# A hybrid mLSTM and Hyena block on one core: operand places of the MLP opened at the start, heads begun beside the last values matmuls, and a new order at the border to the output projection

## The chip, the cores and the metric

The kernel runs on one core of a Trainium2 chip. The metric is device time in microseconds (us) of one execution; before the change three runs took 2702.84, 2704.43 and 2706.27, so the median is 2704.43. The engines are called by their short names: PE (TensorE, matmuls), DVE (VectorE), ACT (ScalarE), POOL (GpSimd) and SP (SyncE, which here only issues loads).

## What the kernel computes

One encoder layer over 2048 positions and 1024 channels in fp32. One projection feeds two groups of 512 channels. Group A is a bidirectional mLSTM with 4 heads of 128 channels, computed in 16 chunks of 128 positions; group B is an order-2 Hyena operator, two long convolutions with gates. Both are normalised per group, joined, projected by `w_out`, normalised and added to the input; a squared-ReLU MLP follows.

```
proj  = rms_norm(x, norm_mix_pre) @ w_in
cv    = short_conv3(proj[:, :N_CONV])              # q, k, hyena v, x1, x2
q, k  = silu(cv[q]), silu(cv[k]) / sqrt(128)       # 4 heads each
v, o  = proj[v], sigmoid(proj[o])
h_m   = (mlstm(q, k, v, gates) + reversed(mlstm(reversed ...))) * o
y_m   = group_rms(h_m, 4)
# mlstm, per chunk: C <- decay*C + (w*k)^T v ;  num = ((q k^T) * wts) v + scale * (q C)
#                   out = num / max(|den|, exp(-m))
z     = cv[x1] * fftconv(cv[hv], filt1);  z = cv[x2] * fftconv(z, filt2)
y_h   = group_rms(z, 8)
x     = x + rms_norm(concat(y_m, y_h) @ w_out, norm_mix_post)
x     = x + rms_norm(relu(rms_norm(x) @ w_mlp_in)^2 @ w_mlp_out, norm_mlp_post)
```

## The kernel before

A fp32 matmul of large size is three matmuls of rounded halves (`mm3`, L159 to L161); the halves are made by ACT (the rounded high part) and DVE or POOL (the rest), in `split` (L166, L169). Small products (mLSTM, transposes) are single fp32 matmuls.

The stages follow one another: normalisation and filters (to 260 us), the first long convolution beside the convolved projections (to 640), the second beside the values projection (to 1024), the mLSTM (to 1168), the output projection (to 1440) and the MLP.

*The stages up to 1024 us* run under a fixed order: every engine takes its instructions as the program writes them. `drive` lets the long convolution lead: each `yield n` of `hyena` asks for n us of projection work, which `convolved` and then `values_project` give in pieces (`yield 1.4` is twelve matmuls, half of a 128x260 tile). Three `yield 1.3` stand in each of its 32 steps j. `values_project` takes four groups of 260 columns in the order 3, 0, 1, 2, each for 16 row tiles t; the normalised input `hn` lies in SBUF for it in four blocks b of 512 rows. Of group 2 (the last) all columns pass a sigmoid on ACT on their way to `vst` and to DRAM `vo`. After the second convolution the lead waits (`yield 14`, then for the gates) and turns head 0's `k`.

*The mLSTM* (`mlstm`, L881) is written as a loop over n = 16 h + ch, and a scheduler places its instructions on each engine. Per chunk there are the score matmul `pS` (L990), the two weight masks `mb` (loaded and broadcast from DRAM `mrow`, cut by POOL at L980 and L981, exponentiated by ACT at L993), their product `pm` on DVE, and, five chunks later, the state product `ps` (L1008) and the two value products `pa` (L1010); ACT scales `ps` into `nm` (L1015), DVE adds `pa`. After each four chunks POOL divides and adds the directions (`ht`, L1028 and L1030), and ACT's queue stores `ym`. Each head needs four groups of transposes `ptk` (L945) with scalings `kw` and fifteen state steps `pv` (L966) first; those of head h+1 stand inside head h. PSUM has five banks for `pv`, `ps`, `pa`, three others for `ptk` and `pS`. The loads of `k`, `q`, `v` are issued by the table `LOADS`; `loads_ahead` loads `w_out` and the data of two gates, `first_gate` makes row tile 0's Hyena half of the output projection's input.

*The output projection* (`out_proj`, L1319) has 16 row tiles of 128 rows. Each takes 48 matmuls `po`: 24 for its Hyena half (`y`, from `gate` and `turned`), 24 for its mLSTM half (`ym`, from `mixed`: POOL's product with the output gate, squares on ACT, sums on DVE, POOL's scaling, transposes). Its opening splits the eight blocks of `w_out` (`weight`, L1339) and prepares rows 0 and 1. From then on a fixed order holds, which works three row tiles at a time.

*The MLP* reads its operands from places `hm<i><e>` of 8 KB per partition, in a pool that is opened after the mLSTM.

## Time and profile before

| | us |
|---|---|
| median of three runs | 2704.43 |
| the profiled execution | 2700.58 |
| its span | 2698.5 |
| PE busy | 2598.6 (96%) |
| DVE, ACT, POOL busy | 1541.0, 1230.1, 1206.1 |
| 0 to 1024 us, PE busy | 994.88 of 1024 |
| 1024 to 1196 us, PE busy | 141.60 of 172 |
| 1196 to 1440 us, PE busy | 236.72 of 244 |
| 1440 to 2698 us, PE busy | 1225.36 of 1258 |

The busy times of the stages are sums of windows of the trace. Times of single instructions are read from the profiled execution, whose clock starts at its first instruction; they carry over to the median only as differences. PE's matmuls overlap by a little, so the spacing of starts tells more than the length of one.

### The profile page before, as it was taken

Reading aid. Unit: us, or ns where it says so; the run is one execution under the profiler, and the core shown is the slowest. Engines: PE = TensorE matmul, PEld = TensorE weight load, DVE = VectorE, ACT = ScalarE, POOL = GpSimd, SP = SyncE. Lnnn points to the kernel's source line nnn. Section 1 sums busy time; section 2 is a strip of 40 time slices with the busy share of each in tenths; the row PEclk is TensorE's granted clock in tenths of the full one; section 3 lists DMA queues with packets and bytes.
Section 4 is the critical chain, followed back from the end, with each engine's and each line's share of the span. In section 5 each row is a group of like instructions: output and inputs, shape, how many; then the busy total and the mean of one; then the engine's idle time right before and its main releaser. Section 6 shows DMA issues by size and latency. Waiting matters only on the chain.

```text
span 2698.5 us, 35390 instructions
## 1 busy us (share of the span) xinstructions
PE 2598.6 (96%) x12237; PEld 2109.2 (78%) x12237; DVE 1541.0 (57%) x2454; ACT 1230.1 (46%) x2292; POOL 1206.1 (45%) x964
## 2 busy tenths in 40 slices
PE   6999999999999998879997999999999999999998
PEld 4778888777798888757774788868888888888876
DVE  5676653777556666656556444474444433543477
ACT  6355544555544446643334444454544333232344
POOL 1211114555225543456667877687772340301232
PEclk9999999999999999899999999999999999999999
DMA  6233336666676658546755444555447453445555
GB/s 173 56 93 110 113 117 216 187 196 187 198 237 180 197 167 272 183 152 213 245 186 210 156 141 163 185 190 172 144 156 282 146 181 98 129 144 160 183 168 214
DMA packets 288354, 465.74 MB, mean 173 GB/s; under 512 B 37542, under 2 KB 149414, under 8 KB 287152
## 3 DMA queue, kind: packets, MB, share of 16 engines
q1 hardware_dynamic: 227600, 324.85, 39.0%
q10 hardware_dynamic: 53264, 117.53, 11.4%
q0 software_dynamic: 7312, 21.11, 3.1%
q8 instruction: 97, 1.59, 0.2%
q14 instruction: 81, 0.66, 0.1%
HBM read 289.27 MB, written 174.13 MB: 172 GB/s over the span
## 4 chain that ended last, share of the span: by engine, by line
PE 39%; DVE 4%; POOL 4%; issue 3%; DMA 2%; ACT 2%; ACTq 0%; DVEq 0%; SPq 0%; POOLq 0%
PE pm L159 13%; PE pm L160 13%; PE pm L161 13%; DMA m<-in_w_mlp_out_dram 1%; POOL xt L1255 1%; DVE cb L169 1%; POOL cb L169 1%; ACT xo L1395 1%; DVE hm L1892 0%; DVE hm L169 0%; DVE xo L1398 0%; DMA hm<-ht 0%; DVE gss L1297 0%; POOL ht L1430 0%; DVE hm L1822 0%
## 5 line engine op out<-in xcount | busy, mean ns | idle before, releaser
L166 ACT CAST cb<-m 128x1024 fp32r<-128x1024 f32 (+1 forms) x342 | 277.4, 846 | 441.3 <-PE pm L159 386.2
L169 DVE TENSOR_TENSOR cb<-m,cb 128x1024 fp32r<-128x1024 f32 (+1 forms) x222 | 237.3, 1106 | 303.1 <-ACT cb L166 302.6
L160 PE MATMUL pm<-cb 128*128 128x512 f32 x880 | 343.4, 390 | 7.8 <-DVE cb L169 7.8
L159 PE MATMUL pm<-cb 128*128 128x512 f32 x880 | 342.3, 389 | 1.3 <-DVE cb L169 1.0
L159 PE MATMUL pm<-hm,cb 128*128 128x512 f32 x840 | 331.4, 394 | 12.3 <-DVE m L1703 6.4
L161 PE MATMUL pm<-cb 128*128 128x512 f32 x880 | 342.5, 389 | 0.0
L160 PE MATMUL pm<-hm,cb 128*128 128x512 f32 x840 | 330.2, 393 | 2.5 <-POOL hm L169 2.5
L161 PE MATMUL pm<-hm,cb 128*128 128x512 f32 x840 | 329.7, 393 | 0.0
L169 POOL TENSOR_TENSOR cb<-m,cb 128x1024 fp32r<-128x1024 f32 x120 | 266.1, 2230 | 57.5 <-ACT cb L166 57.5
L1703 DVE TENSOR_TENSOR m<-pm,m 128x512 f32<-128x512 f32 x224 | 153.9, 690 | 229.4 <-PE pm L161 220.5
L159 PE MATMUL pt<-hn,w 128*128 128x512 f32 x640 | 269.5, 421 | 1.0 <-ACT hn L486 0.9
L160 PE MATMUL pt<-hn,w 128*128 128x512 f32 x640 | 253.9, 397 | 0.7 <-DVE hn L487 0.7
L161 PE MATMUL pt<-hn,w 128*128 128x512 f32 x640 | 253.0, 395 | 0.0
L169 POOL TENSOR_TENSOR raw<-raw,hi 128x512 fp32r<-128x512 f32 x160 | 206.1, 1301 | 99.7 <-ACT hi L166 74.8
L160 PEld LDWEIGHTS pm<-cb 128*128 128x128 f32 x880 | 165.2, 188 | 45.7 <-DVE cb L169 11.7
L159 PEld LDWEIGHTS pm<-hm,cb 128*128 128x128 f32 x840 | 159.2, 189 | 49.0 <-POOL cb L169 7.6
L159 PEld LDWEIGHTS pm<-cb 128*128 128x128 f32 x880 | 165.1, 188 | 36.5 <-ACT junk L1877 1.4
L161 PEld LDWEIGHTS pm<-cb 128*128 128x128 f32 x880 | 165.2, 188 | 33.9
L160 PEld LDWEIGHTS pm<-hm,cb 128*128 128x128 f32 x840 | 159.4, 190 | 37.4 <-POOL hm L169 2.9
L161 PEld LDWEIGHTS pm<-hm,cb 128*128 128x128 f32 x840 | 159.2, 190 | 34.2
L1707 ACT ACTIVATE m<-m 128x512 f32<-128x512 f32 x128 | 80.7, 630 | 229.1 <-DVE m L1703 221.7
L635 POOL DMA_DIRECT2D vp<-vst x96 | 61.2, 642 | 231.7 <-ACT vst L631 230.6
(320 smaller groups left out, 5725.6 us busy)
## 6 DMA issues: line engine op xcount, KB each, us to landing
ga<-m ACTq DMA_DIRECT2D x96, 512.0 KB, 3.6
m<-ga SPq DMA_DIRECT2D x96, 512.0 KB, 3.8
d<-st ACTq DMA_DIRECT2D x64, 512.0 KB, 3.2
m<-in_w_mlp_in_dram SPq DMA_DIRECT2D x64, 512.0 KB, 5.7
m<-in_w_mlp_out_dram SPq DMA_DIRECT2D x114, 256.0 KB, 4.0
raw<-d SPq DMA_DIRECT2D x96, 256.0 KB, 2.9
xt<-in_x_dram SPq DMA_DIRECT2D x32, 512.0 KB, 3.9
dk<-kst SPq DMA_DIRECT2D x32, 512.0 KB, 4.0
```

Source lines behind the costliest of these rows:

```text
L159: pe.matmul(ps, w[1], x[0], start=first, stop=False)
L160: pe.matmul(ps, w[0], x[1], start=False, stop=False)
L161: pe.matmul(ps, w[0], x[0], start=False, stop=last)
L166: self.act.copy(hi, src)
L169: (eng_lo or self.dve).tensor_tensor(lo, src, hi.bitcast(F32), ALU.subtract)
L635: pool.dma_start(dst[:, 8 * b + e:8 * b + 8:2, cc:cc + 128], st[64 * e:64 * e + 64])
L1255: eng.tensor_tensor(res[:, cs], tmp[e], res[:, cs], ALU.add)
L1395: act.activation(x1, xt, AF.Square, accum_out=ss1[:, h:h + 1])
L1703: dve.tensor_tensor(dst, a, b, ALU.add)
L1707: act.activation(g, g, AF.Relu)
```

## The change

Eight of the MLP's operand places (`hm40` to `hm71`, 8 KB each) are opened at the start of the kernel and first hold blocks 0 and 1 of `hn` (now in halves of 4 x 512). When the last values group has used a block, its places take `k`, `q`, `v` and masks of heads 0 and 1, then, inside the mLSTM, operands of head 3, and half of `w_out`. The loads for that stand beside the last values group, at tiles 4 to 15. The transposes, the fifteen state steps and the first scores of head 0 stand there too. The cover of the long convolutions is 1.2 instead of 1.3. In the mLSTM masks are loaded three quads (four chunks each) ahead, and the tables `TURNS`, `WEIGHTS`, `AHEAD` and `GATES` say at which n transposes, splits of `w_out`, loads and two gates come. The opening of the output projection gets a fixed order. Line numbers of the kernel after the change are larger (`ptk` L968, `pv` L989, `pS` L1023, exponentials L1026, `ps` L1041, `pa` L1043, `nm` L1048, sigmoids L736).

```diff
+            self.hq = c.enter_context(tc.tile_pool(name="hq", bufs=1, reuse_waits="tile"))
-            self.hn = [[hp.tile([128, 8, 512], F32R, name=f"hn{b}{e}") for e in range(2)] for b in range(4)]
+            self.hn = [[[self.place(t) for t in tags[2 * e:2 * e + 2]] for e in range(2)]
+                       for tags in (("60", "61", "50", "51"), ("70", "71", "40", "41"))]
+            for b in range(2, 4):
+                self.hn.append([[hp.tile([128, 4, 512], F32R, name=f"hn{b}{e}{j}") for j in range(2)] for e in range(2)])
...
@@ long_conv, after hyena
-        self.mh = [{} for _ in range(4)]
-        self.head_loads(0, "kvq")
-        yield 14.0
-        while not self.gates_done:
-            yield 1.0
-        for g in (0, 3, 1, 2):
-            self.turned(0, g)
-            yield 2.5
+        yield 1.4
+        for i, g in enumerate((0, 3, 1, 2)):
+            self.turned(0, g, ("kt", "s")[i % 2])
+            yield 1.4
+        for step in range(15):
+            self.state_step(0, step, self.mps0, ("s", "kt")[step % 2])
+            yield 1.4
+        for n in range(4):
+            self.scores(0, n)
+            yield 1.4
@@ values_project
+        first = {4: (self.head_loads, 0, "k"), 5: (self.head_loads, 0, "v"), 6: (self.weights_load, 0), 7: (self.head_loads, 0, "q"),
+                 8: (self.weights_load, 1), 9: (self.head_loads, 1, "k"), 10: (self.masked, 0), 11: (self.head_loads, 1, "v"),
+                 12: (self.masked, 1), 13: (self.weights_load, 2), 14: (self.weights_load, 3), 15: (self.head_loads, 1, "q")}
...
+            if g == order[-1] and t in first:
+                first[t][0](*first[t][1:])
@@ mlstm
-        LAG, AHEAD = 5, 10
-        LOADS = {1: "v1", 5: "q1", 9: "k2", 14: "v2", 19: "q2", 32: "k3", 32 + LAG: "v3", 40: "q3"}
+        LAG = 5
+        LOADS = {4: (2, "k"), 8: (2, "v"), 12: (2, "q"), 28: (3, "v"), 32: (3, "k"), 37: (3, "q")}
...
+        GATES = {58: (0, 0), 59: (1, 0), 60: (0, 1), 61: (1, 1), 64: (0, 2), 66: (0, 3), 67: (1, 3)}
-        for step in range(15):
-            self.state_step(0, step)
-        for n in range(64 + LAG):
+        for n in range(4, 64 + LAG):
...
-            while ready < 16 and ready <= (n + AHEAD) // 4:
-                self.weights(*divmod(ready, 4))
+            if n % 4 == 1 and 4 <= n // 4 + 3 < 16 and n > 8:
+                self.weights_load(n // 4 + 3)
...
+            if n % 4 == 3 and n // 4 + 1 < 16:
+                self.masked(n // 4 + 1)
+            if n in WEIGHTS:
+                self.weight(4 + WEIGHTS.index(n))
@@ hyena, three times in a step
-                    yield 1.3
+                    yield 1.2
@@ new: the split of a block of w_out, now also called inside the mLSTM
+    def weight(self, k):
+        hi, lo = (e[:, k % 2, :] for e in self.wos[k // 2])
+        wf = self.ahead.pop(k)
+        self.act.activation(hi, wf, AF.Copy, scale=self.yw[:, k:k + 1])
+        self.dve.scalar_tensor_tensor(lo, wf, self.yw[:, k:k + 1], hi.bitcast(F32), ALU.mult, ALU.subtract)
@@ out_proj, opening
-        for k in (4, 5, 6, 7):
-            weight(k)
-            if k == 5:
-                zs[1] = gate(1)
...
-        ym = {0: turned(mixed(0), 0, 1)}
-        for k in range(4):
-            weight(k)
+        with tc.manual_schedule(engines={mybir.EngineType.PE,mybir.EngineType.DVE,mybir.EngineType.Activation}):
+            opened[2] = opening(2)
+            tiles = mixed_loads(0)
+            pos[0], pos[1] = banks(0), banks(1)
+            for k in (4, 5, 6, 7):
+                weight(k - 4)
+                for i in range(2):
+                    for e in range(2):
+                        part(pos[i], e, yz[i], 4, (k - 4,))
+                if k == 5:
+                    zs[2] = gate(2)
+            yz[2] = yz[0]
+            self.turn_split(ps.tile([128, 512], F32, tag="tp", name="ptp", bufs=3), zs.pop(2), yz[2])
+            pos[2] = [self.h1p.tile([128, 512], F32, tag="h1", name="po1"), ps.tile([128, 512], F32, tag="tp", name="po2", bufs=3)]
+            for e in range(2):
+                part(pos[2], e, yz[2], 4)
+            ym = {0: turned(mixed(0, tiles), 0, 1)}
```

The order on PE at the end of the values projection (`pt`), before:

```order
L160 MATMUL pt_10305<-w1_9562,hn30_94 128x260
L161 MATMUL pt_10305<-w0_9561,hn30_94 128x260
L945 MATMUL ptk_10335<-eye_62,k_10286 128x128 x4
L945 MATMUL ptk_10347<-eye_62,k_10286 128x128 x4
L966 MATMUL pv_10428<-v_10288,kw0_10340 128x129
L966 MATMUL pv_10433<-v_10288,kw0_10340 128x129
L966 MATMUL pv_10438<-v_10288,kw0_10340 128x129
L966 MATMUL pv_10443<-v_10288,kw0_10340 128x129
L945 MATMUL ptk_10359<-eye_62,k_10286 128x128 x4
L966 MATMUL pv_10428<-v_10288,kw1_10353 128x129
```

and after the change, first a state step of head 0 with the next piece of the values matmuls behind it:

```order
L989 MATMUL pv_10458<-hm50_10045,kw0_10211 128x129
L989 MATMUL pv_10458<-hm50_10045,kw1_10185 128x129
L159 MATMUL pt_10443<-w0_9733,hn311_105 128x260
L160 MATMUL pt_10443<-w1_9734,hn301_103 128x260
L161 MATMUL pt_10443<-w0_9733,hn301_103 128x260
```

The end of the values matmuls after the change, further down on the same engine:

```order
L160 MATMUL pt_10443<-w1_9738,hn301_103 128x260
L161 MATMUL pt_10443<-w0_9737,hn301_103 128x260
L989 MATMUL pv_10478<-hm50_10045,kw0_10159 128x129
L989 MATMUL pv_10478<-hm50_10045,kw1_10134 128x129
L989 MATMUL pv_10485<-hm50_10045,kw0_10159 128x129
L989 MATMUL pv_10485<-hm50_10045,kw1_10134 128x129
L989 MATMUL pv_10490<-hm50_10045,kw0_10159 128x129
L989 MATMUL pv_10490<-hm50_10045,kw1_10134 128x129
L1023 MATMUL pS_10495<-hm61_10126,hm60_10003 128x128 x4
L968 MATMUL ptk_10548<-eye_62,hm70_10231 128x128 x3
L1023 MATMUL pS_10539<-hm61_10126,hm60_10003 128x128 x2
L968 MATMUL ptk_10548<-eye_62,hm70_10231 128x128
```

Before, head 0's transposes, all its state steps and its scores come behind the last `pt`. After, three state steps and the scores are what is left of it there; `ptk_10548`, from `hm70`, is already head 1's.

The order on ACT at the same place, before, from the last store of the convolution (`d21`) on:

```order
L234 DMA d21_3601<-st_10228 128x1024
L720 ACTIVATE vst_10245<-pt_10232 128x260
L720 ACTIVATE vst_10318<-pt_10264 128x260
L720 ACTIVATE vst_10318<-pt_10305 128x260
L950 ACTIVATE kw0_10340<-ptk_10335,qt_3582 128x128 x4
L950 ACTIVATE kw0_10352<-ptk_10347,qt_3582 128x128 x4
L950 ACTIVATE kw0_10364<-ptk_10359,qt_3582 128x128 x4
L950 ACTIVATE kw0_10376<-ptk_10371,qt_3582 128x128 x4
L993 ACT_TABLE_LOAD
L993 ACTIVATE mb_10407<-mb_10407,qt_3582 128x128 x8
```

and after:

```order
L1026 ACT_TABLE_LOAD
L1026 ACTIVATE hm51_10084<-hm51_10084,qt_3592 128x128
L973 ACTIVATE kw0_10184<-ptk_10179,qt_3592 128x128 x4
L736 ACT_TABLE_LOAD
L736 ACTIVATE vst_10204<-pt_10140 128x260
L973 ACTIVATE kw0_10211<-ptk_10206,qt_3592 128x128 x4
L736 ACTIVATE vst_10204<-pt_10191 128x260
L1026 ACT_TABLE_LOAD
L1026 ACTIVATE hm51_10084<-hm51_10084,qt_3592 128x128 x4
L736 ACT_TABLE_LOAD
L736 ACTIVATE vst_10296<-pt_10241 128x260
L1026 ACT_TABLE_LOAD
```

The exponentials (of `hm51`, where the masks of quads 0 and 1 lie) have moved between the sigmoids of the last values tiles (`vst`), and a table load stands at each change between them; there are 13 in the tail, where one stood before.

The order on PE at the mLSTM's end, before; `xg0` and `rda` are the Hyena halves of rows 0 and 1, `po0` and `po1` banks of the output projection:

```order
L1008 MATMUL ps_11917<-st_11385,q_11419 128x258
L1010 MATMUL pa_11918<-v_11316,pm_11858 128x129 x2
L1306 MATMUL pty_11922<-eye_62,xg0_10395 128x128 x4
L1290 MATMUL py_11976<-rda_11742,s1i_3586 128x512
L159 MATMUL po0_11992<-wo0_11960,y01_10397 128x512
L159 MATMUL po1_11993<-wo0_11960,y01_10397 128x512
L160 MATMUL po0_11992<-wo1_11961,y00_10396 128x512
L161 MATMUL po0_11992<-wo0_11960,y00_10396 128x512
```

The same place after the change:

```order
L1043 MATMUL pa_11930<-v_11146,pm_11888 128x129 x2
L1350 MATMUL pty_11934<-eye_62,xg0_10525 128x128 x4
L1041 MATMUL ps_11944<-st_11401,hm71_11328 128x258
L1043 MATMUL pa_11945<-v_11146,pm_11888 128x129 x2
L1350 MATMUL pty_11949<-eye_62,rda_11753 128x128 x4
L1041 MATMUL ps_11960<-st_11401,hm71_11328 128x258
L1043 MATMUL pa_11961<-v_11146,pm_11888 128x129 x2
L159 MATMUL po0_12012<-hm60_11362,y01_10521 128x512
L160 MATMUL po0_12012<-hm61_11363,y00_10520 128x512
L161 MATMUL po0_12012<-hm60_11362,y00_10520 128x512
```

Before, row 1's gate (`py`) and the first block of w_out stand at the border; after, both rows' transposes stand in front of the last `pa` and row 0's matmuls directly behind it. Where row 0's mLSTM half (`yt`, from `ymt`) begins, before:

```order
L160 MATMUL po1_12027<-wo1_11963,yt_12018 128x512
L161 MATMUL po1_12027<-wo0_11962,yt_12018 128x512
L1306 MATMUL ptp_12066<-eye_62,ymt_12052 128x128 x4
L1290 MATMUL py_12114<-rd_12109,s1i_3586 128x512 x2
L159 MATMUL po0_11992<-wo0_11964,yt_12065 128x512
L160 MATMUL po0_11992<-wo1_11965,yt_12065 128x512
```

and after:

```order
L159 MATMUL po2_12093<-hm50_11364,y01_10521 128x512
L160 MATMUL po2_12093<-hm51_11365,y00_10520 128x512
L161 MATMUL po2_12093<-hm50_11364,y00_10520 128x512
L1350 MATMUL ptp_12128<-eye_62,ymt_12008 128x128 x4
L159 MATMUL po0_12012<-hm70_11995,yt_12127 128x512
L160 MATMUL po0_12012<-hm71_11996,yt_12127 128x512
```

Before, the transposes of `ymt` stand behind row 1's Hyena half (`po1_12027`), and after behind row 2's (`po2_12093`).

## Rows read from the trace of the kernel before

**Rows 1.** windows: length, busy us of five engines, clock, DMA share, GB/s
```profile
640.00:1024.00 384.00, 379.22 (x2315) 326.20 (x2313) 236.56 (x423) 179.35 (x362) 156.64 (x155) 1.00 0.63 194
1024.00:1044.00 20.00, 14.32 (x94) 13.29 (x93) 10.94 (x35) 11.71 (x38) 3.73 (x7) 0.83 1.00 325
1044.00:1168.00 124.00, 107.78 (x728) 97.09 (x729) 84.27 (x229) 82.28 (x286) 60.98 (x62) 0.94 0.60 187
1168.00:1196.00 28.00, 19.50 (x67) 13.99 (x66) 17.64 (x22) 12.95 (x19) 12.63 (x8) 0.82 0.61 189
1196.00:1385.00 189.00, 187.70 (x871) 145.40 (x870) 109.16 (x193) 73.12 (x183) 118.14 (x107) 1.00 0.66 216
```

**Rows 2.** timeline of PE: start us, us, instruction, [idle before <- releaser]
```profile
1023.39 0.28 PE L161 MATMUL pt<-w,hn 128*128 128x260 f32 x1
...
1043.93 0.67 PE L1008 MATMUL ps<-st,q 128*128 128x258 f32 x2 [1.60 <-DVE st L971]
```

**Rows 3.** timeline of TensorE, a stretch of the mLSTM without waits
```profile
1067.41 0.60 PE L1008 MATMUL ps<-st,q 128*128 128x258 f32 x2
...
1068.52 0.60 PE L1008 MATMUL ps<-st,q 128*128 128x258 f32 x2
```

**Rows 4.** timeline of TensorE, just after it in the mLSTM
```profile
1078.40 0.60 PE L945 MATMUL ptk<-eye,k 128*128 128x128 f32 x4
1078.84 0.61 PE L966 MATMUL pv<-v,kw 128*128 128x129 f32 x4
1079.29 0.39 PE L990 MATMUL pS<-q,k 128*128 128x128 f32 x2
1083.10 1.23 PE L1008 MATMUL ps<-st,q 128*128 128x258 f32 x2 [3.43 <-ACT nm L1015]
```

**Rows 5.** waits from 1023 to 1165 us: us in total, times, longest
```profile
POOL mb L980 <- DMA mb<-mrow: 42.1, 9, 22.0
...
ACT nm L1015 <- POOL ht L1030: 18.4, 8, 4.3
```

**Rows 6.** groups by line, 1023 to 1168 us: busy us, mean ns, idle
```profile
L993 ACT ACTIVATE mb<-mb,qt 128x128 f32<-128x128 f32 x128 | 42.4, 405 | 9.1 <-POOL mb L980 3.7 <-POOL ht L1030 3.3 <-DVE st L971 2.1
...
L1015 ACT ACTIVATE nm<-ps,qt 128x129 f32<-128x129 f32 x126 | 38.9, 373 | 29.7 <-POOL ht L1030 18.4 <-PE ps L1008 9.7 <-PE pa L1010 1.6
...
L950 ACT ACTIVATE kw<-ptk,qt 128x128 f32<-128x128 f32 x64 | 18.3, 376 | 9.8 <-PE ptk L945 9.7
```

**Rows 7.** timeline of ScalarE at the first exponentials
```profile
1036.71 1.28 ACT L993 ACT_TABLE_LOAD   x1
1038.00 4.20 ACT L993 ACTIVATE mb<-mb,qt 128x128 f32<-128x128 f32 x14
```

**Rows 8.** timeline of TensorE from the mLSTM's end into the output projection
```profile
1165.06 1.02 PE L1290 MATMUL py<-rda,s1i 128*128 128x512 f32 x2
...
1166.82 0.61 PE L1010 MATMUL pa<-v,pm 128*128 128x129 f32 x4
...
1180.38 0.40 PE L160 MATMUL po<-wo,y 128*128 128x512 f32 x1
1180.61 0.39 PE L161 MATMUL po<-wo,y 128*128 128x512 f32 x1
...
1185.65 0.80 PE L159 MATMUL po<-wo,yt 128*128 128x512 f32 x1 [4.21 <-DVE yt L169]
...
1193.72 0.60 PE L1306 MATMUL ptp<-eye,ymt 128*128 128x128 f32 x4
...
1195.72 0.55 PE L159 MATMUL po<-wo,yt 128*128 128x512 f32 x1
```

**Rows 9.** timeline of GpSimd, the first normalised ymt
```profile
1186.95 1.99 POOL L1300 TENSOR_TENSOR ymt<-ymt,gr_r 128x512 f32<-128x512 f32 x1 [2.11 <-DVE gr_r L241]
```

**Rows 10.** timeline of VectorE in the second hyena pass
```profile
1005.16 0.68 DVE L1147 TENSOR_TENSOR z<-pu,z 64x512 f32<-64x512 f32 x1 [2.96 <-PE pu L161]
...
1011.70 0.68 DVE L1147 TENSOR_TENSOR z<-pu,z 64x512 f32<-64x512 f32 x1 [2.96 <-PE pu L161]
```

211 lines of the change are left out of this document (111 added, 100 removed).

## The prediction

> **What bounds the kernel now.** I read the windows first, stage by stage [rows 1]. From 640 to 1024 us TensorE is busy 379.22 of 384 us, and in the projection loop after 1196 it is busy 187.70 of 189: both are bound by TensorE. Between them it is not. From 1024 to 1044 it works 14.32 of 20 us with a granted clock of 0.83, from 1044 to 1168 107.78 of 124 at 0.94, from 1168 to 1196 19.50 of 28 at 0.82. Only these 172 us can give anything back, and of the two levels (1.2 and 2.4 GHz) the lower one is in force in part of each.
>
> Then TensorE's timeline at the border [rows 2]: the last matmul of the values projection starts at 1023.39, the first `ps` of the mLSTM at 1043.93. In a run without waits one chunk (pS, ps, pa) costs 1068.52 - 1067.41 = 1.11 us [rows 3]; a group of four transposes `ptk` costs 0.44 and a state step (a pair of `pv`; a step and a group stand in a row) 1078.84 to 1079.29, so 0.45 [rows 4]. The next row there is a `ps` that came 3.43 us late for ACT's `nm`, and it ran 1.23 us where the same shape took 0.60: a stall is paid a second time in the clock. What ACT waited for stands in the table of waits [rows 5]: `nm` waits 18.4 us for GpSimd's `ht`, and GpSimd's masks `mb` wait 42.1 us for their loads, 22.0 of them once, at the start.
>
> **The change, part by part.** *Head 0 beside the last values.* In before all of the mLSTM's TensorE work lies between 1023.5 and the end of the last `pa`, 1166.82 + 0.45 = 1167.3 [rows 2, 8]: 143.8 us. The work is 64 chunks x 1.11 = 71.0, 16 groups of transposes x 0.44 = 7.0, 60 state steps x 0.45 = 27.0 and two gates' `py` at 1.02 [rows 8] = 2.0: 107.0 us, so 36.8 us are lost to waits and the lower clock. After the change 4 groups and 12 of head 0's 15 steps stand between the values' matmuls, where TensorE is full: the values end 4 x 0.44 + 12 x 0.45 = 7.2 us later, at 1030.7. What is left behind is 71.0 + 12 x 0.44 + 48 x 0.45 + 2.9 (two gates with their transposes) = 100.8 us. With no loss the last `pa` ends at 1131.5, 35.8 us earlier; with the old loss at 1168.3, 1.0 later. Neither end is likely. For a gain speaks that the 22.0 us wait for the first masks falls before the values' end, and that the other 20 us of mask waits, which stand behind ACT's 18.4, go when masks are fetched three quads ahead and masked one quad ahead. Against the whole of it speaks ACT's own work [rows 6]: 120 of 128 exponentials (39.8), all `nm` (38.9), three quarters of `kw` (13.7), together 92.4 us, and the casts of half of w_out and of two gates on top: about as much as TensorE's 100.8. Two queues equally full, that wait on each other every chunk, lose something. I take half of the old loss, 18.4 us: last `pa` at 1150, a gain of **17** (-1 to 36).
>
> *Table loads.* The order shows 12 more table loads on ACT in the values' tail, since the exponentials of head 0 now alternate with the sigmoids of the last values. One took 1.28 us and the first exponential started at its end [rows 7]: 12 x 1.28 = 15.4 us of ACT. ACT evicts one 260-wide tile for each 3 to 4 us of TensorE there, so I cost them at nothing on TensorE's path before the border and count what ACT still owes at it into the half loss above; without that cover they cost up to 15.4. The Trainium skill, "ScalarE: Activation LUTs", section "What ACT_TABLE_LOAD costs", gives about 1283 ns for the load and 1380 ns of drain; the trace agrees on the load and shows no drain in front of the exponential. By that page 12 switches would be an estimated 32 us of ACT, 16.6 more for rival C, and the rule to do all of one table set before switching, in its section "Rules for kernel authors", speaks against this order.
>
> *Opening of the output projection.* From the last `pa` (1166.82) to row 0's first mLSTM-half matmul (1195.72) before takes 28.9 us [rows 8]. Half of w_out and both first gates now are split inside the mLSTM, so the 48 matmuls of rows 0 and 1 follow the last `pa` at once, and 24 of row 2 with their transposes come behind. What then is late is the chain of the last `ym`: GpSimd's normalised `ymt` is done at 1186.95 + 1.99 = 1188.94 [rows 9], 22.1 us behind the last `pa`. From the transposes of `ymt` to row 0's matmul it takes 1195.72 - 1193.72 = 2.00 [rows 8], so that matmul starts 24.1 us behind the last `pa`, 4.8 earlier. In that time 24 x 0.23 = 5.5 us of row 2 (1180.38 to 1180.61, the spacing of `po` [rows 8]) are done in addition, which the full loop then banks. Gain **10**. ACT still has the squares of the second `ymt` in front of the cast that row 2 needs (this order made before wait 4.21 us for `yt` [rows 8]): if row 2 slips behind the chain, only 4 remain; if the chain itself, relieved of four splits on VectorE and ACT, shortens by some 6, 16.
>
> *Cover in the long convolution.* 1.2 instead of 1.3 per third of a step keeps up to 0.3 us x 64 = 19 us of projection work for later. It is the same work, so its place costs nothing if TensorE doesn't wait. VectorE's product chain repeats every 1011.70 - 1005.16 = 6.54 us and waits 2.96 us of it for TensorE's `pu` [rows 10]: it has ten times the 0.3 to give. Cost 0, at worst 19. Loads, the doubled mask of one quad, and the split operand places cost nothing: more DMAs on SP's queue, but they come at the end of the hyena's own loads, and TensorE's queue there holds values matmuls whose operands are in place.
>
> **The sum.** 17 + 10 = 27 us off the profiled execution, whose span of 2698.5 makes 2700.58 us: 2673.6. It lies 3.85 under the median of the three runs, so on the median scale 2704.43 - 27 = 2677.
>
> **The rivals.** *A, the work changes its place and the loss stays.* The mLSTM loses 36.8 us as before, since it is ACT and VectorE that are full. For it: ACT's 92.4 us and more. Against: the named waits for masks. Only the opening is gained: 2704.4 + 1.0 - 10 = 2695.
>
> *B, the stalls vanish.* A loss of 5 us and the short chain: 31 + 14 = 45 us, 2659. Against it stands ACT again.
>
> *C, slower: ACT's queue at the border.* In the tail ACT runs in order through exponentials of masks that are loaded late there (the order has quads 2 and 3 behind the stores of vst), each between two table loads. If a mask comes as late as the first one in before, 22.0 us, ACT's sigmoids, `kw` and `nm` stand behind it, and 15.4 us of loads with them: up to 37.4 us, that TensorE can't bridge, since its banks for `ps` are freed by ACT's `nm` alone. From 27 us of ACT's lag it is a loss; at its full size 2677 + 37 = 2714. Against: TensorE reads no sigmoid, and the masks' loads move out of the 20 us in which the DMA engines were full (share 1.00) into a stage at 0.63 [rows 1].
>
> *D, the cover was needed.* Each hyena step waits for what it lost: up to 19 us, 2696. Against: the 2.96 us of slack above.
>
> **How the numbers follow.** Forecast 2677 with chance 0.52 (its own range 2666 to 2690: losses of 8 to 28 us, with openings of 10 and 6). A 0.17, B 0.08, C 0.10, D 0.13. 0.2% of the time, 5.4 us, is about what can be told from no change. Faster: all of the forecast and B, most of A (9 us, 0.145) and of D (0.10): 0.85. Same: what is left of A and D with a small C, 0.07. Slower: C and the worst of D, 0.08. Leaving 0.1 out above and 0.1 below, the range is 2662 to 2698.
>
> **What would show it.** Right: a first `ps` within 3 us of the last values matmul, at about 1033; the last `pa` near 1150; waits of GpSimd's masks far under 42 us; row 0's mLSTM half some 24 us behind the last `pa`, with row 2's hyena half in front of it; hyena steps of about 6.25 us without new waits. Wrong: a last `pa` beyond 1160 (A), TensorE waiting for `nm` behind table loads around 1035 (C), waits for `pu`, `pi` or `py` between 300 and 1000 us (D), or the MLP's 1258 us changed, on which I count nothing.

## The result: slower by 0.3%, where 1% faster was forecast

The changed kernel takes 2712.68 us (median of 8 runs, 2711.35 to 2717.36), the kernel before beside it 2706.09 (8 runs, 2701.78 to 2707.16). The ratio is 1.0029 with a 95% interval of 1.0019 to 1.004. The forecast was 2677, with a range of 2662 to 2698.

The profiled execution has a span of 2709.8 us against 2698.5, so 11.3 more; the medians are 6.6 apart, so a single pair of traces holds some us of scatter. The windows of the kernel after, same columns as [rows 1]:

```profile
640.00:1024.00 384.00, 378.69 (x2304) 326.15 (x2303) 238.79 (x435) 189.24 (x384) 155.59 (x154) 1.00 0.65 204
1024.00:1044.00 20.00, 15.15 (x117) 14.43 (x116) 7.91 (x19) 16.77 (x32) 4.26 (x10) 0.93 0.80 255
1044.00:1168.00 124.00, 107.12 (x732) 94.90 (x731) 90.06 (x239) 86.93 (x286) 63.85 (x59) 0.98 0.58 175
1168.00:1196.00 28.00, 21.58 (x84) 16.25 (x84) 7.92 (x11) 5.83 (x10) 9.27 (x8) 0.88 0.48 161
1196.00:1385.00 189.00, 182.66 (x841) 141.84 (x840) 107.37 (x191) 73.37 (x183) 116.67 (x106) 0.98 0.65 213
```

The three windows that could give something back run at a higher clock, as meant, and two of them are a little fuller (the one from 1044 to 1168 is not: 107.12 against 107.78). But the loop after 1196, full before (187.70 of 189), is not any more (182.66). A table by fixed times does not show the rest, so I cut the trace at TensorE's own marks: the end of the last values matmul, the end of the last `pa`, the start of TensorE's first `pm` (the MLP's matmuls; VectorE's `pm` in the mLSTM is another tile), the end of the last `pm`. Worked out from the traces, in us, differences from unrounded times:

```
                          before    after    difference
values end                1023.7   1031.8       +8.1
values end -> last pa      143.8    129.6      -14.1
last pa -> first pm        249.0    253.2       +4.1
first pm -> last pm       1272.7   1285.9      +13.2
rest                         9.3      9.3        0
```

So the mLSTM gains 14.1 us behind the values' end, 8.1 of which the values pay, 4.1 are lost again in the output projection, and 13.2 in the MLP, whose code the change does not touch.

TensorE at the border in after (start, us, instruction, [idle before <- releaser]), to be held against [rows 2, 8]:

```profile
1031.52 0.28 PE L161 MATMUL pt<-w,hn 128*128 128x260 f32 x1
...
1034.83 0.60 PE L1041 MATMUL ps<-st,hm 128*128 128x258 f32 x2
...
1041.88 1.23 PE L1043 MATMUL pa<-hm,pm 128*128 128x129 f32 x4 [3.35 <-DVE pm L1029]
...
1160.84 0.61 PE L1043 MATMUL pa<-v,pm 128*128 128x129 f32 x4
```

The first `ps` comes 3.3 us behind the last values matmul instead of 20.5, but the first `pa` only 10.1 us behind the values' end: it needs the product `pm` of the scores and masks of chunks 0 to 3, and so their exponentials. ScalarE there, first its timeline, then the mask's cut on GpSimd and the product on VectorE:

```profile
1020.57 0.39 ACT L736 ACTIVATE vst<-pt 128x260 f32<-128x260 f32 x1 [1.17 <-issue]
1026.30 1.28 ACT L1026 ACT_TABLE_LOAD   x1 [5.34 <-DMA hm<-mrow]
1027.59 0.40 ACT L1026 ACTIVATE hm<-hm,qt 128x128 f32<-128x128 f32 x1
1028.01 1.28 ACT L736 ACT_TABLE_LOAD   x1
1029.31 0.39 ACT L736 ACTIVATE vst<-pt 128x260 f32<-128x260 f32 x1
...
1036.83 1.28 ACT L1026 ACT_TABLE_LOAD   x1
1038.12 2.44 ACT L1026 ACTIVATE hm<-hm,qt 128x128 f32<-128x128 f32 x8
```
```profile
1026.35 0.64 POOL L1013 TENSOR_SCALAR_AFFINE_SELECT hm<-hm 128x512 f32<-128x512 f32 x1 [19.12 <-DMA hm<-mrow]
```
```profile
1040.60 1.23 DVE L1029 SCALAR_TENSOR_TENSOR pm<-pS,hm 128x1024 f32<-128x1024 f32 x1 [3.29 <-ACT hm L1026]
```

That is rival C in small: a mask comes late (5.34 us), sigmoids and exponentials alternate, and 13 table loads of 1.28 us stand between 1005 and 1038. The late mask is that of chunk 8, and the eight exponentials of chunks 0 to 3 are the last row of ScalarE: in its order they stand behind those of chunks 4 to 9, though the first `pa` needs them first. The waits from 1023 to 1165 us, as in [rows 5]:

```profile
POOL hm L1013 <- DMA hm<-mrow: 19.1, 1, 19.1
POOL mb L1013 <- DMA mb<-mrow: 13.3, 4, 4.9
...
ACT nm L1048 <- POOL ht L1063: 9.1, 5, 2.3
PE pa L1043 <- ACT nm L1048: 8.2, 8, 1.8
```

ScalarE's wait for `ht` halved (18.4 to 9.1). It did not vanish, and what it really is comes below.

### The profile page after: what moved, and what is told of

Same layout as the page of the kernel before. It is cut to its first block, busy times and chain, and to the rows that moved or that the text cites. A ratio compares the mean times of both kernels' runs of the same rounds, so it can differ in the third digit from the quotient of the medians.

```text
span 2709.8 us, 35397 instructions
## 1 busy us (share of the span) xinstructions
PE 2606.8 (96%) x12237; PEld 2108.6 (78%) x12237; DVE 1552.2 (57%) x2453; ACT 1242.7 (46%) x2303; POOL 1209.3 (45%) x964
## 3 DMA queue, kind: packets, MB, share of 16 engines
q10 hardware_dynamic: 53264, 117.53, 11.3%
## 4 chain that ended last, share of the span: by engine, by line
PE 39%; DVE 4%; POOL 4%; DMA 3%; issue 3%; ACT 2%; ACTq 0%; SPq 0%; DVEq 0%; POOLq 0%
PE pm L159 13%; PE pm L161 13%; PE pm L160 13%; DVE cb L169 1%; POOL xt L1288 1%; POOL cb L169 1%; DMA hm<-ht 1%; ACT xo L1448 1%; DVE hm L1946 0%; POOL ht L1483 0%; DVE gss L1341 0%; DMA m<-in_w_mlp_in_dram 0%; DVE m L1757 0%; DVE xo L1451 0%; DVE hm L169 0%
## 5 line engine op out<-in xcount | busy, mean ns | idle before, releaser
L646 POOL DMA_DIRECT2D vp<-vst x96 | 61.2, 642 | 233.0 <-ACT vst L642 231.9
L612 DVE SCALAR_TENSOR_TENSOR yc<-pt,cw,yc 128x511 f32<-128x511 f32 (+1 forms) x280 | 135.1, 516 | 45.2 <-ACT yc L606 43.1
L1861 POOL TENSOR_TENSOR m<-m,hm 128x512 f32<-128x512 f32 x32 | 50.1, 1568 | 241.1 <-DMA m<-in_w_mlp_out_dram 230.1
L159 PE MATMUL pt<-hm,w 128*128 128x512 f32 x320 | 133.2, 416 | 0.9 <-ACT hm L494 0.9
```

The costliest lines, as they stand in the source:

```text
L159: pe.matmul(ps, w[1], x[0], start=first, stop=False)
L612: dve.scalar_tensor_tensor(y[:, at], p[:, src], cw[:, ct, w:w + 1], y[:, at], ALU.mult, ALU.add)
L646: pool.dma_start(dst[:, 8 * b + e:8 * b + 8:2, cc:cc + 128], st[64 * e:64 * e + 64])
L1861: pool.tensor_tensor(b[:, 0], b[:, 0], t2[s], ALU.subtract)
```

## Experiments

Two theories stood at the start. Theory 1: the MLP's 13 us come from the tiles' new addresses; its rival: from the new order, by way of the clock or of transfers. Theory 2: the mLSTM's gain fell short for the masks' late loads; its rivals: the table loads, ScalarE's work, and the queues. Times are of the slowest core, "before" is the kernel before, run beside it. As a first finding of all these runs together: the time of the values' end differs between kernels whose code up to there is the same (1023.1 to 1027.9 in seven built on before, 1031.8 to 1037.5 in five that are after up to there), so stages are compared by their length and not by times from the start. The lengths scatter too. Where the code of a stage is after's, the stretch from the values' end to the last `pa` takes 129.6 to 132.9 us, and the MLP at after's addresses 1281.7 to 1286.8. Runs for which no interval is given are single executions.

**b_layout: before with after's addresses.** The change has two side effects on SBUF: the decay tile went from the right-hand side into the constants on the left (128 bytes more there), and two operand places of the MLP became 8256 bytes wide, for v with its 129th column.

```diff
-            self.cp_bg = cp.tile([128, 16], F32, name="bg")
-            self.cw = cp.tile([128, 20, 4], F32, name="cw")
+            t = cp.tile([128, 128], F32, name="cw")
+            self.cp_bg, self.cw = t[:, 80:96], t[:, 0:80].rearrange("p (t n) -> p t n", n=4)
+            self.decay = t
...
-        wos = {j: [wp.tile([128, 2, D], F32R, tag=f"hm{i}{e}", ...
+        wos = {j: [wp.tile([128, 2, D] if e or i > 5 else [128, 16, 129], F32R, tag=f"hm{i}{e}", ...
```

> The kernel before with one thing changed: its MLP tiles lie at the SBUF addresses that they have after the change (the shared cw/bg/decay tile at the bottom, two operand places of 8256 instead of 8192 bytes, so that operands, raw ring and split weights move by 128 to 512 bytes). Order and work are those of before. Theory 1 (the addresses slow the MLP's up steps): an up step of 84 matmuls takes 19.3 to 19.5 us instead of 19.05, the MLP is 7 to 9 us longer over its 32 up steps, and the whole run is 6 to 11 us slower than before. Rival (the MLP is slower because of what the new order leaves behind: stalls, clock, queues): 19.05 us a step and a time within 3 us of before.

Measured: 2714.94 against 2705.41, ratio 1.0035 (1.0024 to 1.0047). Its MLP takes 1284.1 us, and its matmuls have after's spacing to the tenth of a nanosecond. Addresses alone, with before's order of instructions, are as slow as the whole change.

**b_decay: the decay tile alone.**

> The kernel before with only the decay tile moved into the shared tile at the bottom: left-hand tiles (operands hm4 to hm7, hm3, ring) 128 bytes up, right-hand tiles (split weights, hm1, hm2) 512 bytes up. Theory 1: the up steps leave 19.05 us if distances between left and right tiles matter (they change by 384 bytes); they stay if only the widened places matter. Rival: 19.05 us, time as before.

Measured: 2712.74; MLP 1283.0. The 128 bytes of the decay tile are enough, with another pattern of slow products.

**a_right256: after with 256 bytes of padding on the right** (one unused tile under places 1 and 2).

> The changed kernel with a pad of 256 bytes in front of the right-hand MLP tiles, so that ring and split weights have the distance of the kernel before again (modulo 512 bytes), and hm3 too; hm4 to hm7 have not. Theory 1 in the form 'ring against split weights': up steps back to 19.05 to 19.15 us and the run 6 to 9 us faster than the changed kernel (2704 to 2707). In the form 'hm4 to hm7 against something': steps stay at 19.4 and the time at 2712. Rival (order, not addresses): 19.4, 2712.

Measured: 2715.82, ratio to before 1.004 (1.0025 to 1.0054), the spacing as after's. I took it for proof that right-hand addresses don't count. That was too quick: 256 turned out to be the one padding that can't show anything.

**a_masks: after with the mask rows loaded earlier** (rows 2 and 3 at tiles 9 and 11, head 1's k and v behind them).

> The changed kernel with the loads of masks 2 and 3 four and three tiles earlier (tiles 9 and 11 of the last values group) and head 1's k and v later (13 and 14). Theory 2 (ACT stood 5.3 us behind a late mask in the values' tail, and TensorE then 1.5 + 3.4 us behind ACT, at a lower clock): those waits at 1037 to 1042 us go and the last pa is 4 to 8 us earlier. Rival (the mLSTM is full on ACT and VectorE, so it is given back): the last pa is less than 2 us earlier. Either way the MLP is as in the changed kernel.

Measured: 2716.96, ratio 1.0039 (1.0024 to 1.0054); 132.3 us from the values' end (1035.35) to the last `pa` against 129.6. No gain. ScalarE's longest wait for a mask in the tail is 1.58 us now, and yet the first `pa` comes 9.2 us behind the values' end. On ScalarE, VectorE and TensorE:

```profile
1040.75 2.44 ACT L1026 ACTIVATE hm<-hm,qt 128x128 f32<-128x128 f32 x8
```
```profile
1043.22 1.22 DVE L1029 SCALAR_TENSOR_TENSOR pm<-pS,hm 128x1024 f32<-128x1024 f32 x1 [2.37 <-ACT hm L1026]
```
```profile
1044.50 0.71 PE L1043 MATMUL pa<-hm,pm 128*128 128x129 f32 x4 [2.43 <-DVE pm L1029]
```

The exponentials of chunks 0 to 3 are again the last of the tail, now behind those of chunks 4 to 12. Theory 2 falls in this form: the late mask alone does not hold the start.

**b_ring256, b_hm128, a_ring256: which tile?** One unused tile ahead of the ring of result tiles, or ahead of the operand places:

```diff
+            mk.tile([128, 64], F32, tag="pad", name="pad")          # b_ring256, a_ring256
+            self.hq.tile([128, 32], F32, tag="pad", name="pad")     # b_hm128
```

> Kernel before with one unused 256-byte tile ahead of the MLP's ring of result and weight tiles, so that this ring alone lies 256 bytes higher (at the address it has after the change); operand places, constants and right-hand tiles stay. Theory ring (the distance between ring and other tiles sets the spacing of the up steps' matmuls): products 1, 2, 6, 5, 7 of the first 16 steps go from 226.7 to some 231 to 233 ns, time about 2713 (+7 to +9). Theory places (the moving operands' own address does): spacing as before (226.7, with 5 at 228.2 and 7 at 232.4), time about 2705.

> Kernel before with one unused 128-byte tile ahead of the operand places, so that places 3 to 7 and the ring behind them lie 128 bytes higher; constants and right-hand tiles stay. Theory places and theory ring both: as the run that moved the decay tile alone, products 1, 2, 6 at 233.3 and 5 at 232.4 ns, time about 2712. Rival (the constants' tiles, which that run moved too, or the right-hand side): spacing as before, about 2705.

> Kernel after with the same 256-byte tile ahead of the ring, which then stands at its address of before plus 512 bytes. Theory ring, if the address counts modulo 512: spacing of before comes back, time about 2704 (-9). Theory places: spacing as after, about 2713.

Measured: b_ring256 2707.4 with before's spacing, a_ring256 2714.11 with after's, b_hm128 2711.76 with b_decay's. The ring is out; the moving operands' places are what counts. Sorting the up steps' matmuls by product (mean spacing in ns, steps 3 to 14, 12 matmuls of 512 columns each; in brackets the address of the place, high and low part, in bytes modulo 256; the stationary weights stand at 160 in all but b_right128, where they stand at 32):

```
product      1           2           6           5           7           4           3
before       227.9 (160) 226.7 (160) 226.7 (160) 226.7 (160) 226.7 (160) 226.7 (160) 232.6 (32)
b_hm128      226.7 (160) 226.7 (160) 232.6 (32)  233.3 (32)  233.3 (32)  233.3 (32)  227.9 (160)
after        230.8 (160) 226.7 (160) 232.6 (32)  231.7 (32,96) 232.9 (96) 233.0 (96,160) 231.7 (32)
b_right128   226.7 (32)  226.7 (32)  232.6 (160) 233.3 (160) 233.3 (160) 233.3 (160) 227.9 (32)
a_align      226.7 (160) 226.7 (160) 226.7 (160) 226.7 (160) 226.7 (160) 226.7 (160) 226.7 (160)
```

A product is fast where its moving and its stationary operand stand at the same byte modulo 256, and slow where they don't; the first two or three matmuls of a product still show the one before it (227.9). Two things do not fit a rule of each matmul by itself: product 1 of after has both at 160 and takes 230.8, slow in ten of its matmuls behind the slow product 3; and in its product 4 the four matmuls that read the low part, at 160 like the weights, take 234.8 ns on the mean, no less than the eight that read the high part at 96. Why stays open. The last two rows were run to test the sentence.

**b_right128 and a_align.** 128 bytes on the right-hand side of before move weights and places 1 and 2 to 32; in a_align all places and the weights of after stand at 160 (two unused 64-byte tiles; place 40 first, its operand 64 bytes into the slot). b_align is before with 128 bytes ahead of place 3.

```diff
+            hm = {t: self.place(t) for t in ("40", "60", "61", "51", "70", "71", "41", "50")}   # a_align
...
+            t = self.hq.tile([128, 2064], dtype, tag="hm40", name="hm40")[:, 16:2064]
```

> Kernel before with one unused 128-byte tile on the right-hand side, so that the split weights (the up steps' stationary operands) and places 1 and 2 go from 160 to 32 bytes modulo 256; places 3 to 7 stay (place 3 at 32, the others at 160). Theory pair (a matmul is slow where its moving and its stationary operand lie at different bytes modulo 256): products 6, 5, 7, 4 go to 232 to 233 ns, 1, 2 and 3 to 226.7; up steps some +0.2 us each, time about 2712. Theory moving (a moving operand at 32 is slow wherever the weights are): products 1, 2, 3 at 232 to 233, 6, 5, 7, 4 at 226.7; time about 2709.

> Kernel before with one unused 128-byte tile ahead of place 3, which goes from 32 to 160 bytes modulo 256, as do the output projection's yt, yz and the ring. Theory pair: product 3 falls from 232.6 to 226.7 ns (12 matmuls by 5.9 ns in 30 up steps: 2.1 us less) and the output projection's matmuls from 232 to 227 (768 by 5 ns: up to 3.8 us where PE bounds them); time 2700 to 2703, ratio to before about 0.998. Theory moving: product 3 falls as well, the output projection's matmuls do not; time 2703.

> Kernel after with all operand places of the MLP and the output projection, and the ring, at 160 bytes modulo 256 (place 40 first, as a slot of 8256 bytes with its operand 64 bytes in, unused 64-byte tiles ahead of place 40 and of place 3). Theory pair and theory moving: all up products at 226.7 ns, the up steps take back their 8 us and 2 more; time about 2702 (2699 to 2706), ratio to before 0.998 to 1.0. If the up steps stay slow, addresses modulo 256 are not what counts.

Measured: b_right128 2715.26, with exactly the products slow that the pair rule names: products 1, 2 and 3, whose places now stand at 32, are fast, because the weights stand there too. The rule that the moving operand's address alone counts falls. The profile shows it in start times of TensorE's timeline: first and last matmul of products 1 and 7 in b_right128, of product 7 in after, and of the same in a_align.

```profile
1553.96 0.39 PE L159 MATMUL pm<-hm,cb 128*128 128x512 f32 x1
...
1556.46 0.39 PE L161 MATMUL pm<-hm,cb 128*128 128x512 f32 x1
...
1564.99 0.40 PE L159 MATMUL pm<-hm,cb 128*128 128x512 f32 x1
...
1567.57 0.39 PE L161 MATMUL pm<-hm,cb 128*128 128x512 f32 x1
```
```profile
1559.28 0.39 PE L159 MATMUL pm<-hm,cb 128*128 128x512 f32 x1
...
1561.84 0.40 PE L161 MATMUL pm<-hm,cb 128*128 128x512 f32 x1
```
```profile
1563.42 0.39 PE L159 MATMUL pm<-hm,cb 128*128 128x512 f32 x1
...
1565.91 0.39 PE L161 MATMUL pm<-hm,cb 128*128 128x512 f32 x1
```

Eleven spacings make 2.50 us in product 1 of b_right128 and 2.58 in its product 7, 2.56 in after and 2.49 in a_align. No wait stands in any of these rows: what is lost is in the spacing of the matmuls itself. a_align takes 2702.85 (10 runs), its MLP 1273.4 instead of 1285.9; ratio to before 0.9998 (0.9986 to 1.001). b_align: 2702.84, 0.9992 (0.9981 to 1.0003). So without its addresses the change is worth nothing measurable either way.

**a_proj, b_proj: the same rule in the projections?** There 1920 matmuls of 512 columns run at 232.5 ns, and their weights lay at eight different bytes modulo 256. I meant to put all four parts of a column block into one tile, at 160 as the moving operands.

```diff
-            w = [self.pw.tile([128, 520], F32R, tag=f"w{e}", name=f"w{e}", bufs=4)[:, 0:nk * n] ...
+            if i % 2 == 0:
+                self.wt = self.pw.tile([128, 2080], F32R, tag="w", name="w", bufs=2)
+            o = (i % 2) * 2 * L + (32 if L == 512 and i // 2 % 2 == 0 else 0)
```

> Kernel before with place 3, yt and yz at 160 bytes modulo 256 as in the run above, and the projections' split weights of a column block (two chunks, hi and lo) in one tile so placed that all four stand at 160 too, as the moving operands hn do (they stood at eight different residues). Theory pair: the projections' 1920 matmuls of 512 columns fall from 232.4 to 226.7 ns, up to 11 us where TensorE bounds the stage; time 2692 to 2700, ratio to before 0.995 to 0.998. If the pair rule holds for the MLP alone: spacing in the projections as before, time about 2703.

> Kernel after with the same layout of the projections' weights and all MLP and output-projection operands at 160 bytes modulo 256 except place 40 (product 4's high part, at 96). Theory pair: the projections' matmuls at 226.7 ns, up products at 226.7 but for 4; the stage up to the values' end some 5 to 11 us shorter; time 2692 to 2703. Otherwise as the run with aligned places, about 2703 to 2705.

Measured: the spacing stays (232.7 and 232.4), b_proj takes 2708.73 (1.0011, 1.0001 to 1.0021), a_proj 2709.65 (1.0012, 1.0002 to 1.0021). But the edit did not do what it was meant to. In the programs that ran, the parts of 512 columns stand at 32 modulo 256 in both buffers of their tile, and `hn` at 160 (in a_proj a few at 96). So every one of these matmuls has an unequal pair, and 232.7 ns lies where the rule has it (232.6 to 233.3 in the MLP). Equal bytes were not tried in the projections: whether the rule holds there stays open. In a_proj's MLP the high part of product 4's place stands at 96; product 4 takes 233.0 and product 3 behind it, at 160 with both operands, 230.3. The rule holds for whole products of the MLP. In the output projection medians of 227 instead of 231 to 232 ns agree with it (a_align and b_align against after and before).

**a_mixed: where the output projection gives the lead back.** TensorE's opening in after:

```profile
1180.66 0.66 PE L1350 MATMUL ptp<-eye,yz 128*128 128x128 f32 x4 [2.42 <-POOL yz L1344]
...
1183.92 0.80 PE L159 MATMUL po<-hm,y 128*128 128x512 f32 x1 [2.60 <-DVE y L169]
...
1193.47 0.50 PE L159 MATMUL po<-hm,yt 128*128 128x512 f32 x1 [1.40 <-DVE yt L169]
...
1217.39 1.12 PE L1350 MATMUL ptp<-eye,ymt 128*128 128x128 f32 x4 [4.88 <-POOL ymt L1344]
```

Counted in `po` matmuls behind the last `pa`, after is ahead of before by 9.7 us at the 48th (16.8 against 26.5) and still by 5.3 at the 120th (48.9 against 54.2), and behind by 4.5 at the 144th (65.2 against 60.7). Between the 120th and the 144th lie the last of these rows, a wait of 4.88 us, and a stretch at the lower of the two clock levels (granted 0.50, 1.2 GHz):

```profile
1215.40:1222.20 6.80, 4.81 (x14) 3.95 (x15) 3.40 (x9) 3.04 (x9) 5.54 (x5) 0.50 0.64 200
```

GpSimd's `ymt` is late there since ScalarE squares row 3's `ymt` behind row 0's norm. a_mixed calls it ahead. (`mixed(3)` makes row 3's mLSTM half; the expectations call it the Hyena half.)

```diff
+                    if i == 1:
+                        ys[3] = mixed(3)
                     xns[i - 1] = normed(i - 1, *done)
```

> Kernel after with row 3's Hyena half (its square on ScalarE) called ahead of row 0's norm in the turn of the loop where the lead is given back. Theory (the 4.88 us wait of the turn at 1217.39 and the half clock behind it are that order's): the wait shrinks to under 1.5 us, first MLP matmul 4 to 7 us earlier than after's 1414.6. Rival (the loop's steady 14.55 us a row takes it back anyway): first MLP matmul within 1 us of after's.

Measured: the wait shrinks to 1.00 us and a_mixed is at 58.6 at the 144th matmul. But the next turn then waits, in a_mixed:

```profile
1231.41 0.66 PE L1350 MATMUL ptp<-eye,yz 128*128 128x128 f32 x4 [2.47 <-DVE xo L1462]
```

and at the 168th it is at 71.0 (after 73.3, before 68.8). From the last `pa` to the first `pm` 251.3 instead of 253.2: 1.9 us, under half of what I expected, and a_scores below, without this edit, takes 250.8. So the wait is that order's, but that its going brings the MLP's start forward is not shown. (Its one time, 2719.47, holds a late values' end and after's MLP.)

**a_scores: is it the mLSTM's start?** The scores of head 0's first four chunks are called behind the values instead of between them.

```diff
-        for n in range(4):
-            self.scores(0, n)
-            yield 1.4
...
+        for n in range(4):
+            self.scores(0, n)
         for n in range(4, 64 + LAG):
```

> Kernel after with the scores of head 0's first four chunks (4 matmuls and 8 exponentials on ScalarE) called after the values' last tile instead of between its last tiles. Theory alternation (the 13 table loads between sigmoids and exponentials hold the mLSTM's start): 2 loads are left, the first pa comes 3 to 4 us earlier behind the values' end (10 us now), and the stretch from the values' end to the last pa falls from 130 to 126 us. Rival (the stretch is bound by what a chunk costs, and the start is made up within the first chunks): the first pa earlier, the stretch within 1 us of 130.

Measured: 2714.23. Half a miss. The order on ScalarE did not become what I expected: 15 table loads stand there and not 2. But none of them waits for a mask any more, the exponentials of chunks 0 to 3 come first (the last of them ends at 1021.2), and the first `pa` comes 3.8 us behind the values' end instead of 10.1. a_masks has 15 loads there and no late mask either, and its first `pa` comes at 9.2. What the two differ in is the order: in a_scores these eight exponentials, and the scores and products that go with them, come first. So their place behind the others held the start; a late mask and table loads count as far as they stand in front of them. The stretch to the last `pa` stays all the same, 130.8: after 36 of the 64 chunks a_scores is still 5.3 us ahead of after (72.8 against 78.1 behind the values' end), after 38 it is 2.1 behind. There, on TensorE and then on ScalarE:

```profile
1104.96 0.49 PE L1042 MATMUL pa<-v,pm 128*128 128x129 f32 x2 [1.76 <-ACT nm L1047]
...
1111.71 1.23 PE L1040 MATMUL ps<-st,q 128*128 128x258 f32 x2 [3.37 <-ACT nm L1047]
```
```profile
1109.58 0.37 ACTq L234 DMA_DIRECT2D ym<-ht  x1
1110.00 1.14 ACT L972 ACTIVATE kw<-ptk,qt 128x128 f32<-128x128 f32 x4 [4.06 <-POOL ht L1062]
```

Of a_scores' two theories the rival stands: the earlier start is made up again within the stretch.

**a_exp1: is it ScalarE's work?** The kernel leaves out the second direction's own bias.

```diff
-        for d in range(2):
-            col = 64 * d + 16 * h + ch
-            act.activation(mb[:, d, i, :], mb[:, d, i, :], AF.Exp, scale=-1.0, bias=self.qt[:, 0, col:col + 1])
+        col = 16 * h + ch
+        act.activation(mb[:, :, i, :], mb[:, :, i, :], AF.Exp, scale=-1.0, bias=self.qt[:, 0, col:col + 1])
```

> Kernel after in which each chunk's two exponentials (one per direction, each with its own bias) are one instruction of 128x256 with the first direction's bias, so the second direction's masks are not those of the reference. ScalarE loses 64 instructions, some 64 x 0.2 = 13 us of its work in the mLSTM. Theory ACT (the mLSTM's chunks come at the rate of ScalarE's queue): the stretch from the values' end to the last pa falls from 130 to 117 to 122 us. Rival (it is the chain of one chunk group through GpSimd, VectorE and ScalarE that sets the rate): it falls by less than 4 us.

Measured: 2718.42, and 130.1 us from the values' end to the last `pa`. ScalarE's groups by line behind the values' end, first after's, then a_exp1's:

```profile
L1026 ACT ACTIVATE hm<-hm,qt 128x128 f32<-128x128 f32 x70 | 24.5, 417 | 1.9 <-POOL hm L1013 1.5 <-POOL hm L1014 0.4
L1026 ACT ACTIVATE mb<-mb,qt 128x128 f32<-128x128 f32 x48 | 15.8, 410 | 2.1 <-POOL ht L1063 2.1
```
```profile
L1025 ACT ACTIVATE hm<-hm,qt 128x256 f32<-128x256 f32 x32 | 14.7, 520 | 2.3 <-DVE den L1057 1.7 <-POOL hm L1014 0.6
...
L1025 ACT ACTIVATE mb<-mb,qt 128x256 f32<-128x256 f32 x24 | 11.1, 532 | 2.8 <-POOL ht L1062 2.8
```

40.3 us of exponentials became 25.8, and the stretch did not move. ScalarE's load is not the bound; the theory I had forecast by falls.

**a_ymq: the store in ScalarE's queue.** What is left is the row above it: ScalarE issues the store of `ht`, and its queue stands at that issue until GpSimd has made `ht`. The `nm` and `kw` behind it, which need no `ht`, wait with it. So it is in after:

```profile
1105.32 0.37 ACTq L234 DMA_DIRECT2D ym<-ht  x1
1105.73 0.63 ACT L1048 ACTIVATE nm<-ps,qt 128x129 f32<-128x129 f32 x2 [2.01 <-POOL ht L1063]
```

```diff
-            self.store(self.ym[:, 128 * h:128 * h + 128] ..., m["hs"])
+            pool.dma_start(self.ym[:, 128 * h:128 * h + 128] ..., m["hs"])
```

> Kernel after in which the mLSTM's 16 stores ym<-ht are issued by GpSimd, right behind the sum that makes ht, instead of by ScalarE, whose queue stands at the issue until ht is done (rows ACT nm or kw <- POOL ht, 9.1 us in after, 18.4 before). Theory queue (these waits of ScalarE set the mLSTM's rate): they vanish, and the stretch from the first pa to the last falls from 119.5 to 108 to 113 us. Rival (GpSimd's own queue, lengthened by 16 issues of 0.7 to 0.9 us, or the lag between scores and values sets the rate): 117 us or more.

Measured: 2708.96; from the first `pa` to the last 115.0 us against 119.6 (119.3 to 121.5 in the kernels whose mLSTM is after's), between the two theories. ScalarE's waits for `ht` are gone from the table, and those of TensorE's `pa` for `nm` fall from 8.2 us to

```profile
PE pa L1043 <- ACT nm L1048: 1.4, 2, 0.8
```

The place where a_scores fell back is not as quick as in after, though: from the end of chunk 36's `pa` to that of chunk 38's a_ymq takes 9.2 us, a_scores 11.9, after 4.5. How much of that is other work of TensorE and how much waiting was not taken apart.

**a_best and a_best2: the losses mended together.** a_best is a_align with the edits of a_mixed and a_scores, a_best2 has GpSimd's stores too.

> Kernel after with the aligned places, head 0's first scores behind the values' end and row 3's Hyena half ahead of row 0's norm (the three edits tried before, together). By the parts measured one by one: the MLP 12.5 us shorter than after's, the stretch from the last pa to the first MLP matmul 2 to 4 us shorter, the rest as after: 2697 to 2701, ratio to before 0.997 to 0.999. If the three gains don't add, about 2703 and a ratio of 1.0.

> The three edits of a_best and the stores ym<-ht from GpSimd's queue. If the gains add: the stretch from the values' end to the last pa 129.8 to 125 or 126 us, the rest as a_best, so 4 us less than it: ratio to before 0.9965 to 0.998. If the lead is given back in the output projection's opening, whose ymt waits for GpSimd: as a_best, 0.9988.

Measured: a_best 2704.87 (12 runs), ratio 0.9988 (0.9978 to 0.9998): the ratio is what I expected, the time is not (before, run beside it, stood at 2708.36), and the stretch from the last `pa` to the first `pm` is 250.1, no shorter than a_scores' alone by more than 0.7. a_best2 2696.42 (5 runs, 2689.18 to 2700.76) against 2708.11, ratio 0.9959 (0.9945 to 0.9973), a little more than expected. a_best2 is 0.4% faster than before. Its windows:

```profile
1024.00:1044.00 20.00, 18.79 (x153) 18.14 (x152) 8.89 (x22) 19.79 (x41) 4.28 (x10) 1.00 0.87 251
1044.00:1168.00 124.00, 112.12 (x758) 99.99 (x757) 92.66 (x244) 88.57 (x284) 78.81 (x76) 0.99 0.59 192
```

The early start and the free queue need each other: alone, a_scores gave nothing to the last `pa` and a_ymq 3.7 us; together the stretch from the values' end to the last `pa` falls by 10.1 (129.6 to 119.5). a_best is the control: it has all of a_best2 but the stores, and takes 129.8.

## Why the prediction was wrong, step by step

The sum took 27 us off; the profiled execution is 11.3 longer, so 38.3 us are missing. 11.0 of them lie in the mLSTM with the values in front of it (a gain of 6.0 instead of 17), 14.1 in the output projection (a loss of 4.1 instead of a gain of 10), 13.2 in the MLP.

**Head 0 beside the last values: half right.** The values end at 1031.8 (1030.7 was said; this trace is the earliest, others with the same code have 1033.7 to 1037.5), the first `ps` comes at 1034.8 (1033 was said), GpSimd's mask waits fall from 42.1 us to 32.4, most of them now ahead of the border. The loss behind the values' end is 129.6 - 100.8 = 28.8 us, and not the 18.4 that the sum took. The step that failed is its reason: "two queues equally full, that wait on each other every chunk". a_exp1 shows that ScalarE's fullness is not what costs: 14.5 us less of its work moved nothing. What cost was the order in its queue. The exponentials that the first `pa` needs stood last (6.3 us at the start in a_scores, which alone were lost again), and the store of `ht` held those behind it (some 4 us in a_ymq). With both mended the loss is 119.5 - 100.8 = 18.7, which is the half I had taken; that the two agree is luck, since the half had another reason. What makes up these 18.7 was not taken apart. In [rows 5] the store could have been seen: ScalarE's `nm` reads `ps` and not `ht`, so a wait for `ht` can only come from something else in its queue.

**Table loads: right in cost, too simple in effect.** Each took 1.28 us and the exponential or sigmoid started at its end. Fifteen of them in a_scores did not hold the start, so counting them at nothing up to the border was right. In a_masks the first `pa` waits for exponentials that ScalarE reaches only behind 15 loads, with no gap in its work from 1011.3 on. Whether a load counts goes by what stands behind it.

**Opening of the output projection: wrong in sign.** Forecast: row 0's mLSTM half 24.1 us behind the last `pa`, 10 us gained. Measured 1193.47 - 1160.84 = 32.6 (28.9 before): row 2's Hyena half stood in front and waited 2.42 and 2.60 us for its own chain, with the lower clock behind it. GpSimd's normalised `ymt`, forecast 22.1 us behind the last `pa`, was done 25.5 us behind it, at 1186.32 (the row holds both rows' `ymt`),

```profile
1185.28 2.04 POOL L1344 TENSOR_TENSOR ymt<-ymt,gr_r 128x512 f32<-128x512 f32 x2 [3.27 <-DVE gr_r L241]
```

and TensorE, with row 2's half, came to its transposes only at 1191.47. The lead that the early matmuls of rows 0 and 1 had made was given back at one turn of the loop: after takes 9.8 us more than before between the 120th and the 144th matmul, 4.88 of them a wait, some 2.4 (an estimate, half of the 4.81 us that TensorE works in the stretch at half clock) the clock. I had banked a lead without asking which turn of the loop would have its inputs late for it.

**Cover in the long convolution: right, by a reading that was not.** The 6.54 us of [rows 10] are one spacing and not the rhythm. VectorE's products still show it in after,

```profile
986.41 0.68 DVE L1180 TENSOR_TENSOR z<-pu,z 64x512 f32<-64x512 f32 x1 [1.53 <-PE pu L161]
...
992.95 0.68 DVE L1180 TENSOR_TENSOR z<-pu,z 64x512 f32<-64x512 f32 x1 [2.97 <-PE pu L161]
```

but over the second pass its 31 spacings average 5.99 us before and 5.58 after. So the steps became shorter, as meant, and TensorE's waits from 260 us to the values' end are 4.6 us before and 5.3 after. Rival D falls.

**The MLP, "on which I count nothing": 13.2 us.** No term of the sum had it, and of the rivals none. 9.1 us are the addresses: the mean spacings of the seven products add up to 1619.4 ns in after and 1594.0 in before, 25.4 x 12 matmuls x 30 steps. The other 4 lie in its first three steps, where before's trace is a lucky one: b_ring256, with before's order and spacing, takes 92.9 us for them, after 94.8 and before 89.5. That the change costs these 4 is not shown. The Trainium skill, "SBUF — State Buffer", section "Who interferes with whom", says that PE never waits on anyone, and "TensorE: Matmul & The Clock Gate", section "Step-by-step: what each phase is for", that loading the next weights takes no read bandwidth from the running matmul; by both one would expect no cost from the bytes at which operands lie. Here b_hm128 and b_right128 measure 226.7 against 233.3 ns by these bytes alone, and the measurement decides.

Of the rivals, C's queue at the border did hold the first `pa`, by some 6 us and not 37, and A's loss in the mLSTM (36.8 us) is a little nearer to the measured 28.8 than the forecast's 18.4; neither was the reason that the kernel became slower. That was the MLP's addresses: with them mended (a_align) after is level with before.

## What to carry to other kernels

When a change moves or resizes a tile, the addresses of everything behind it in the pool move: compare the spacing of equal matmuls in stages that the change does not touch, and keep moving and stationary operands at one byte modulo 256 where a run shows that it matters. Read in the built program where the tiles of a padded kernel lie; in a_proj and b_proj they did not lie where I thought. Read in each queue what the next stage needs first: here it stood last. The store was better off in the queue of the engine that makes its data; in another's queue it made every instruction behind it wait, and the table of waits then shows an instruction that waits for a tile which it never reads. And a lead at the entrance of a full loop is a gain only if every later turn has its inputs earlier too.
